# A two-block model on one core: experts' weights read by whole 8 KB rows, gate and up in two PSUM banks each, and the second block's small loads issued by ACT

## The chip, the cores and the metric

The kernel runs on one core of a Trainium2 chip. The metric is the device time of one execution, in microseconds (us). The engines are PE (matrix products), DVE, ACT and POOL (elementwise work), and SP, which here only issues transfers; ACT can issue transfers too. The 16 DMA engines of the core move data between the chip's DRAM and SBUF for both queues.

## The reference

Two transformer blocks follow each other on 256 tokens of width 1024, in float32. The first block (272 tokens with 16 meta tokens) has attention and a convolution, then an expert layer: each of 16 experts chooses its 34 best tokens. The second block has four branches, a merge and a plain feed-forward layer. The expert layer is the part that matters here:

```python
def expert_choice_ffn(h, w_router, w_gate, w_up, w_down):
    cap = EC_CAPACITY_FACTOR * L // N_EXPERTS                  # 34
    logits = jnp.einsum('ld,de->le', hs, w_router)
    aff = jax.nn.softmax(logits, axis=-1)
    g, idx = lax.top_k(aff.T, cap)
    xg = hs[idx]                                               # 16 x 34 x 1024
    a = jnp.einsum('ecd,edf->ecf', xg, w_gate)                 # w_gate 16 x 1024 x 2048
    u = jnp.einsum('ecd,edf->ecf', xg, w_up)                   # w_up   16 x 1024 x 2048
    y = jnp.einsum('ecf,efd->ecd', jax.nn.silu(a) * u, w_down) # w_down 16 x 2048 x 1024
    out = jnp.zeros((L, D)).at[idx.reshape(-1)].add((y * g[..., None]).reshape(-1, D))
```

## The kernel before, in words

The program has three stages, one after the other: block 1, the 16 experts, block 2. The order of instructions on each engine is not the order of the code: the framework schedules the program when it is built, by a timeline of its own, and its pools decide which buffer a tile gets.

**Loads of weights.** Every weight matrix is read in pieces of at most 1 MB by `load` (L121, on SP's queue) into a tile `raw` of 128 partitions x 2048 floats, that is 8 KB to a partition. There are 18 such tiles during the experts (12 from the start, 4 and 2 more when block 1 gives up space). A load waits until the tile's last reader is done. It also waits for a semaphore: all transfers of SP's and ACT's queues share eight, named DMAHW0 to DMAHW7 in the program's order, handed out in turn as the scheduler places the transfers, and a transfer waits until the one that had its semaphore before has landed. So no more than eight transfers are on their way, counted over both queues.

**Experts** (`moe`, from L728). `xg` holds the chosen tokens of eight experts, transposed, with 34 columns padded to 64. It is made by `gather` (L715, five products `gat_p` for each of the eight 128-row blocks K of the model width, then a copy to `xg`), once ahead of expert 0 and once inside expert 7. A product of an expert (`pair`, L737) takes 64 columns of `xg` against 1024 weight columns as two products of 512 columns, one into each half of the partitions. For each expert and each half `fh` of the 2048 hidden columns: four loads of `w_gate` (a load holds 256 model rows x 1024 hidden columns), eight pairs into one PSUM bank `pg`; four loads of `w_up`, eight pairs into `pu`; the banks are copied to SBUF (`sg` on ACT, `su` on DVE), transposed on PE (`gT_p`, four 128x128 pieces), passed through Silu on ACT (`sl`) and multiplied on DVE to `hT`. Then eight loads of `w_down` feed 16 pairs into `py`; ACT copies it to `ys`, PE spreads it over the tokens (`cmb_p`), DVE adds it to `hres`. An expert has 24 loads of 1 MB: 8 gate, 8 up, 8 down.

**Small loads of block 2** (`params2`, L851). Norm gains, biases and tables of block 2 are loaded by 21 small transfers on SP's queue. Seven go to tiles of their own (`c_inv`, `r_alog`, `r_dtb`, `r_fb`, `r_gqr`, `r_gkr`, `r_sgb`) and the scheduler places them in block 1. Fourteen reuse tiles that the second `gather` reads last (`c_tri`, eleven rows of `p_rows`, `p_sgw`, `p_pos`) and are placed after it.

Of the kernel before, what the change touches and what calls it, by code (L numbers as in the profile page):

```python
# [7 lines left out]
F32 = mybir.dt.float32  # L8
# [717 lines left out]
def moe(g, pc):  # L726
# [4 lines left out]
    with ExitStack() as c:  # L731
# [7 lines left out]
        for e in range(g.NEXP):  # L739
            if e == 0:  # L740
                places(g, 0)
                gather(g, ps)
                last = weigh(g, 0)
            if e == min(8, g.NEXP - 1):
                with tc.issue_after(last.ins):
                    q2 = params2(g, pc)
            if e == min(10, g.NEXP - 1):
                with tc.issue_after(g.last.ins), tc.issue_after(g.lastv.ins):
                    params2_calc(g, q2, *(ps.tile([128, 512], F32, tag="mt", name="ws_p") for _ in range(2)))

            sT_p = ps.tile([128, 512], F32, tag="mt", name="sT_p")
            for i in range(2):
                for n in range(2):
                    nc.tensor.matmul(
                        sT_p[HALF[n], i * 128 : i * 128 + 128], g.Sg[:, i, e % 8], g.ident, start=True, stop=True
                    )
            sT = wk.tile([128, 256], F32, tag="sT", name="sT")
            nc.vector.tensor_copy(sT, sT_p[:, :256])
            hT = wk.tile([128, 16, 64], F32, tag="hT", bufs=1, name="hT")
            for fh in range(2):  # L760
                for nm, weights in (("g", I["w_gate"]), ("u", I["w_up"])):
                    p = ps.tile([128, 512], F32, tag="p" + nm, bufs=1, name="p" + nm)
                    for kq in range(4):
                        w = load(
                            g,
                            weights[0, e, kq * 256 : kq * 256 + 256, fh * 1024 : fh * 1024 + 1024].rearrange(
                                "(k p) f -> p k f", p=128
                            ),
                            2,
                            1024,  # L770
                        )
                        for kk in range(2):
                            K = kq * 2 + kk
                            pair(p, g.xg[:, K, e % 8], w[:, kk], K == 0, K == 7)
                    s = wk.tile([128, 512], F32, tag="s", name="s" + nm)
                    if nm == "g":
                        nc.scalar.activation(s, p, AF.Copy)  # L777
                    else:
                        nc.vector.tensor_copy(s, p)  # L779
                    pt = ps.tile([128, 512], F32, tag="mt", name="gT_p")  # L780
                    for j in range(4):
                        js = slice(j * 128, j * 128 + 128)
                        nc.tensor.transpose(pt[:, js], s[:, js], g.ident)

                    if nm == "g":
                        sl = wk.tile([128, 512], F32, tag="sl", name="sl")
                        nc.scalar.activation(sl, pt, AF.Silu)
                    else:
                        h = hT[:, fh * 8 : fh * 8 + 8].rearrange("p (n j) c -> p j n c", n=2)
                        pv, sv = (x.rearrange("p (j n c) -> p j n c", j=4, n=2) for x in (pt, sl))  # L790
                        nc.vector.tensor_tensor(h, sv, pv, op=ALU.mult)
            if e == 7:
                places(g, 1)
                gather(g, ps)
                last = weigh(g, 1)
            py = ps.tile([128, 512], F32, tag="py", bufs=2, name="py")
            for q in range(8):
                w = load(g, I["w_down"][0, e, q * 256 : (q + 1) * 256].rearrange("(k p) f -> p k f", p=128), 2, 1024)
                for kk in range(2):
                    K = q * 2 + kk  # L800
                    pair(py, hT[:, K], w[:, kk], K == 0, K == 15)
            ys = wk.tile([128, 512], F32, tag="s", name="ys")
            g.last = nc.scalar.activation(ys, py, AF.Copy)  # L803
            for i in range(2):
                pn = [ps.tile([128, 512], F32, tag="mt", name="cmb_p") for _ in range(2)]
                for n in range(2):
                    ins = nc.tensor.matmul(pn[n], sT[HALF[n], i * 128 : i * 128 + 128], ys[HALF[n]], start=True, stop=True)  # L807
                for n in range(2):
                    d = g.h[:, i, n * 512 : (n + 1) * 512]
                    g.lastv = nc.vector.tensor_tensor(d, pn[n], d, op=ALU.add)  # L810
# [39 lines left out]
def params2(g, pool):  # L850

    nc, I = g.nc, g.I
    q = Ctx()
    dma = nc.sync.dma_start

    def row(name, src, n):
        t = pool.tile([128, n], F32, name="r_" + name)
        dma(t, src.broadcast_to([128, n]))
        return t

    q.inv = load_const(g, pool, "inv")
    q.tri0 = load_const(g, g.rt, "tri", tag="hh1")
    q.rows = g.rt.tile([98, 128], F32, tag="hl0", name="p_rows")
    nc.gpsimd.memset(q.rows, 0.0)
    q.vec = pool.tile([128, 98], F32, name="p_vec")
# [1066 lines left out]
```

## Time and profile before

| what | value |
|---|---|
| median of 3 runs | 1705.66 us (1704.28 to 1706.36) |
| profiled execution, device time | 1703.82 us |
| its span, first to last instruction | 1702.0 us |
| PE busy | 1517.8 us, 89% of the span |
| DVE, ACT, POOL busy | 583.4, 438.8, 128.0 us |
| moved by DMA | 510.65 MB, of which 384 loads of 1 MB are the experts' weights |

The profiled execution is 1.84 us below the median of the runs. The span is the time from the first to the last instruction. The busy time of an engine counts neither its waits nor the transfers that it issues. The profile also has, for each stretch of time, the busy share of the 16 DMA engines, the rate at which they moved data and the clock granted to PE as a part of its full speed.

### The profile page before, as it was taken

How to read it: one execution, taken by the hardware profiler on the slowest of the kernel's cores; microseconds unless marked ns; L12 is line 12 of the kernel's file. 1: busy time of each engine (PE TensorE's matmuls, PEld its weight loads, DVE VectorE, ACT ScalarE, POOL GpSimd, SP SyncE). 2: the span in 40 equal slices, each digit the busy share in tenths (PEclk: the TensorE clock that was granted, in tenths of full speed). 3: DMA queues.
4: the chain of work that ended last, by engine and by line, in shares of the span. 5: the costliest groups of instructions: out<-in, count | busy, mean ns of one | idle time of the engine just before them, and what ended most of it. 6: DMA issues, size and time to landing. Idle time of an engine off the chain costs nothing.

```text
span 1702.0 us, 21226 instructions
## 1 busy us (share of the span) xinstructions
PE 1517.8 (89%) x8652; PEld 889.3 (52%) x8652; DVE 583.4 (34%) x1071; ACT 438.8 (26%) x882; POOL 128.0 (8%) x134
## 2 busy tenths in 40 slices
PE   7999999978878897878888887869999999999999
PEld 6887333222222232222222222228999998989998
DVE  5675111101101110101110110127888765576554
ACT  3544100000000000000000000026677444455543
POOL 2043000000000000000000000010141111220000
PEclk8999999999999999999999999999999999999999
DMA  9746899999999999999999999984442433466653
GB/s 291 230 135 237 323 409 409 409 409 410 409 409 409 409 409 344 409 409 409 408 409 409 409 409 409 409 315 149 151 154 75 149 125 112 137 197 199 197 186 113
DMA packets 189736, 510.65 MB, mean 300 GB/s; under 512 B 10827, under 2 KB 80438, under 8 KB 189638
## 3 DMA queue, kind: packets, MB, share of 16 engines
q1 hardware_dynamic: 188118, 509.01, 79.5%
q8 instruction: 68, 1.11, 0.3%
q10 hardware_dynamic: 1520, 0.28, 0.1%
q14 instruction: 30, 0.25, 0.0%
HBM read 508.21 MB, written 1.05 MB: 299 GB/s over the span
## 4 chain that ended last, share of the span: by engine, by line
PE 45%; DMA 42%; DVE 2%; issue 1%; ACT 0%; POOL 0%; SPq 0%; ACTq 0%; DVEq 0%; POOLq 0%
DMA raw<-in_w_up_dram 28%; DMA raw<-in_w_down_dram 14%; PE pu L737 5%; PE py L737 4%; PE pg L737 3%; PE pA_p L1079 3%; PE pA_p L1081 3%; PE pA_p L1080 3%; PE ff_p L1823 2%; PE ff L1862 2%; PE ff L1861 2%; PE ff_p L1824 2%; PE ff_p L1825 2%; PE ff L1860 2%; PE pB_p L1097 1%; PE pB_p L1099 1%
## 5 line engine op out<-in xcount | busy, mean ns | idle before, releaser
L150 DVE TENSOR_TENSOR wl<-raw,wh 128x1024 fp32r<-128x1024 f32 (+4 forms) x212 | 246.2, 1163 | 128.8 <-ACT wh L148 128.1
L737 PE MATMUL py<-raw,hT 128*64 128x512 f32 x1024 | 244.3, 602 | 47.1 <-DMA raw<-in_w_down_dram 47.1
L737 PE MATMUL pu<-raw,xg 128*64 128x512 f32 x1024 | 248.8, 607 | 41.8 <-DMA raw<-in_w_up_dram 41.5
L148 ACT ACTIVATE wh<-raw 128x1024 fp32r<-128x1024 f32 (+4 forms) x214 | 208.4, 976 | 199.0 <-PE pA_p L1080 42.5
L737 PE MATMUL pg<-raw,xg 128*64 128x512 f32 x1024 | 242.7, 600 | 15.6 <-DMA raw<-in_w_gate_dram 15.6
L737 PEld LDWEIGHTS py<-raw,hT 128*64 128x64 f32 x1024 | 66.2, 136 | 208.4 <-issue 105.8
L779 DVE COPY su<-pu 128x512 f32<-128x512 f32 x32 | 22.1, 692 | 438.5 <-PE pu L737 438.5
L737 PEld LDWEIGHTS pu<-raw,xg 128*64 128x64 f32 x1024 | 65.8, 137 | 199.2 <-DMA raw<-in_w_up_dram 108.5
L810 DVE TENSOR_TENSOR hres<-cmb_p,hres 128x512 f32<-128x512 f32 x64 | 41.2, 686 | 333.5 <-PE cmb_p L807 333.5
L737 PEld LDWEIGHTS pg<-raw,xg 128*64 128x64 f32 x1024 | 66.1, 136 | 159.9 <-issue 109.0
L803 ACT ACTIVATE ys<-py 128x512 f32<-128x512 f32 x16 | 9.6, 597 | 422.1 <-PE py L737 422.1
L777 ACT ACTIVATE sg<-pg 128x512 f32<-128x512 f32 x32 | 19.1, 597 | 376.2 <-PE pg L737 376.2
L1081 PE MATMUL pA_p<-x2h,wl 128*128 128x256 f32 x384 | 109.5, 285 | 0.0
L1079 PE MATMUL pA_p<-x2h,wh 128*128 128x256 f32 x384 | 109.3, 285 | 0.2 <-ACT abk L1722 0.2
L1080 PE MATMUL pA_p<-x2l,wh 128*128 128x256 f32 x384 | 108.1, 281 | 0.0
L1079 PEld LDWEIGHTS pA_p<-x2h,wh 128*128 128x128 f32 x384 | 72.4, 189 | 2.0 <-issue 0.8
L1081 PEld LDWEIGHTS pA_p<-x2h,wl 128*128 128x128 f32 x384 | 72.2, 188 | 2.1 <-issue 1.9
L1080 PEld LDWEIGHTS pA_p<-x2l,wh 128*128 128x128 f32 x384 | 72.3, 188 | 1.1 <-issue 0.8
L1824 PE MATMUL ff_p<-fl,wh 128*128 128x256 f32 x256 | 71.1, 279 | 0.0
L1823 PE MATMUL ff_p<-fh,wh 128*128 128x256 f32 x256 | 70.1, 278 | 0.8 <-ACT fh L1002 0.5
L1825 PE MATMUL ff_p<-fh,wl 128*128 128x256 f32 x256 | 70.5, 277 | 0.0
L461 PE MATMUL proj_p<-xh,wh 128*128 128x272 f32 x192 | 57.4, 313 | 1.9 <-DVE hT L282 1.9
(574 smaller groups left out, 2282.3 us busy)
## 6 DMA issues: line engine op xcount, KB each, us to landing
raw<-in_w_gate_dram SPq DMA_DIRECT2D x128, 1024.0 KB
raw<-in_w_up_dram SPq DMA_DIRECT2D x128, 1024.0 KB
raw<-in_w_down_dram SPq DMA_DIRECT2D x128, 1024.0 KB
raw<-in_w_in_dram SPq DMA_DIRECT2D x43, 1024.0 KB
raw<-in_w_ff_dram SPq DMA_DIRECT2D x32, 1024.0 KB
raw<-in_w_out_dram SPq DMA_DIRECT2D x8, 1024.0 KB
raw<-in_w_branch_dram SPq DMA_DIRECT2D x16, 512.0 KB
raw<-in_w_in_dram SPq DMA_DIRECT2D x4, 512.0 KB
```

What stands on the lines that cost most here:

```text
L148: g.lastw = nc.scalar.activation(h, x, AF.Copy)
L150: ve.tensor_tensor(l, x, h.bitcast(F32), op=ALU.subtract)
L461: ins = nc.tensor.matmul(p[:, :L1], w[:, k, js], x[:, k], start=(n == 0), stop=(n == 23))
L737: nc.tensor.matmul(p[HALF[n]], x, w[:, n * 512 : n * 512 + 512], start=first, stop=last)
L810: g.lastv = nc.vector.tensor_tensor(d, pn[n], d, op=ALU.add)
L1079: nc.tensor.matmul(o, wh[:, k, js], xh[:, k], start=(k == 0), stop=False)
L1080: nc.tensor.matmul(o, wh[:, k, js], xl[:, k], start=False, stop=False)
L1081: nc.tensor.matmul(o, wl[:, k, js], xh[:, k], start=False, stop=(k == 7))
L1823: nc.tensor.matmul(o, wh[:, k, js], fh[:, k], start=(k == 0), stop=False)
L1824: nc.tensor.matmul(o, wh[:, k, js], fl[:, k], start=False, stop=False)
L1825: nc.tensor.matmul(o, wl[:, k, js], fh[:, k], start=False, stop=(k == 7))
L1860: nc.tensor.matmul(o, a[:, TS[t]], wh[:, j, ns], start=(K == 0), stop=False)
```

## The change

It has three parts. Rows: the gate and up loads take 128 whole rows of 2048 floats, so each partition receives one run of 8 KB in place of two runs of 4 KB; the down loads give each partition two neighbouring rows of 4 KB, again one run of 8 KB. Banks: a gate or up load now holds all 2048 hidden columns of one K, so both halves are summed side by side, `pg` and `pu` are two PSUM banks each, all eight gate loads come ahead of all eight up loads, and the copies and transposes of the two halves follow each other; the transposes read `s` in another order, so that the rows of `hT` match the new rows of the down loads. Small loads: all 21 of `params2` are issued by ACT in place of SP.

```diff
-            for fh in range(2):
-                for nm, weights in (("g", I["w_gate"]), ("u", I["w_up"])):
-                    p = ps.tile([128, 512], F32, tag="p" + nm, bufs=1, name="p" + nm)
-                    for kq in range(4):
-                        w = load(
-                            g,
-                            weights[0, e, kq * 256 : kq * 256 + 256, fh * 1024 : fh * 1024 + 1024].rearrange(
-                                "(k p) f -> p k f", p=128
-                            ),
-                            2,
-                            1024,
-                        )
-                        for kk in range(2):
-                            K = kq * 2 + kk
-                            pair(p, g.xg[:, K, e % 8], w[:, kk], K == 0, K == 7)
+            sls = []
+            for nm, weights in (("g", I["w_gate"]), ("u", I["w_up"])):
+
+                p = ps.tile([128, 2, 512], F32, tag="p" + nm, bufs=1, name="p" + nm)
+                for K in range(8):
+                    w = load(
+                        g,
+                        weights[0, e, K * 128 : K * 128 + 128].rearrange("p (a f) -> p a f", a=2),
+                        2,
+                        1024,
+                    )
+                    for fh in range(2):
+                        pair(p[:, fh], g.xg[:, K, e % 8], w[:, fh], K == 0, K == 7)
+                for fh in range(2):
...
+                    sv = s.rearrange("p (m q k) -> p m k q", m=2, k=2)
                     for j in range(4):
-                        js = slice(j * 128, j * 128 + 128)
-                        nc.tensor.transpose(pt[:, js], s[:, js], g.ident)
+                        nc.tensor.transpose(pt[:, j * 128 : j * 128 + 128], sv[:, j // 2, j % 2], g.ident)
...
-                w = load(g, I["w_down"][0, e, q * 256 : (q + 1) * 256].rearrange("(k p) f -> p k f", p=128), 2, 1024)
+                w = load(g, I["w_down"][0, e, q * 256 : (q + 1) * 256].rearrange("(p k) f -> p k f", k=2), 2, 1024)
...
-    dma = nc.sync.dma_start
+
+    dma = nc.scalar.dma_start
...
-    q.inv = load_const(g, pool, "inv")
-    q.tri0 = load_const(g, g.rt, "tri", tag="hh1")
+    q.inv = load_const(g, pool, "inv", eng=nc.scalar)
+    q.tri0 = load_const(g, g.rt, "tri", tag="hh1", eng=nc.scalar)
```

Three places of the built program show what moved. In brackets stands what an instruction waits for; x4 is four equal rows.

The first place is ACT near the start of the program, where `xh` is block 1's input, transposed and scaled. Before:

```order
L251 ACTIVATE sqx,ssx<-hres 128x1024 [waits Pool_49]
L261 ACTIVATE xh<-ptx,mg 128x272 [waits DVE_49,PE_49]
L261 ACTIVATE xh<-ptx,mg 128x272 [waits PE_49] x3
L148 ACTIVATE wh<-raw 128x1024 [waits DMAHW4_49]
L261 ACTIVATE xh<-ptx,mg 128x272 [waits PE_49] x3
```

The same place of ACT after the change:

```order
L251 ACTIVATE sqx,ssx<-hres 128x1024 [waits Pool_49]
L93 DMA c_inv<-in_consts_dram 128x32 [waits DMAHW5_49]
L860 DMA r_alog<-in_dn_a_log_dram 128x4 [waits DMAHW7_49]
L261 ACTIVATE xh<-ptx,mg 128x272 [waits DVE_49,PE_49]
L261 ACTIVATE xh<-ptx,mg 128x272 [waits PE_49]
L860 DMA r_dtb<-in_dn_dt_bias_dram 128x4 [waits DMAHW1_49]
L261 ACTIVATE xh<-ptx,mg 128x272 [waits PE_49] x5
L148 ACTIVATE wh<-raw 128x1024 [waits DMAHW4_49]
L275 ACTIVATE sqx,ssx<-hres 128x1024 [waits DMAHW2_49,Activation_49]
L860 DMA r_fb<-in_fox_f_bias_dram 128x4 [waits DMAHW4_49]
```

Two small loads now stand ahead of the first `xh`, one between them, and four more (`r_fb` to `r_sgb`) ahead of the eighth `xh`.

The second place is expert 8, after the second gather. On SP before, the fourteen small loads stood between the sixth and the seventh load of the second half's rows of `w_up`, each waiting for the semaphore of a transfer eight places ahead:

```order
L121 DMA raw<-in_w_up_dram 128x2x1024 [waits DMAHW5_49,PE_49]
L93 DMA c_tri<-in_consts_dram 128x128 [waits DVE_49,DMAHW6_49,PE_49,Pool_49]
L870 DMA p_rows<-in_norm_g_dram 8x128 [waits DMAHW7_49,Pool_49]
...
L899 DMA p_pos<-in_positions_dram 2x128 [waits DMAHW3_49,PE_49]
L121 DMA raw<-in_w_up_dram 128x2x1024 [waits DMAHW4_49,PE_49]
```

On ACT after the change they stand between the last copy of the gather (`xg`) and `ys` of expert 7:

```order
L896 DMA p_sgw<-in_sg_w_s_dram 128x4x128 [waits DMAHW6_49,PE_49]
L721 ACTIVATE xg<-gat_p,vec 128x8x34 [waits PE_49]
L93 DMA c_tri<-in_consts_dram 128x128 [waits DMAHW7_49]
...
L872 DMA p_rows<-in_mla_q_norm_g_dram 2x128 [waits DMAHW5_49]
...
L901 DMA p_pos<-in_positions_dram 2x128 [waits DMAHW6_49]
L804 ACTIVATE ys<-py 128x512 [waits DVE_49,PE_49]
```

SP after the change has only weight loads there; these are the last three up loads of expert 8 and its first two down loads, with the semaphores left to them:

```order
L121 DMA raw<-in_w_up_dram 128x2048 [waits DMAHW5_49,PE_49]
L121 DMA raw<-in_w_up_dram 128x2048 [waits DMAHW2_49,PE_49]
L121 DMA raw<-in_w_up_dram 128x2048 [waits DMAHW6_49,PE_49]
L121 DMA raw<-in_w_down_dram 128x2048 [waits DMAHW2_49,PE_49]
L121 DMA raw<-in_w_down_dram 128x2048 [waits DMAHW7_49,PE_49]
```

The semaphores missing from this row of loads (3, 4, 5, 7, 0, 1, and so on) went to the small loads of ACT.

The third place is PE in the first gather, where `pg` and `pu` begin (`Sm,hm` is the last of the five gather products of a K, `hh` and `hl` are the high and low part of the tokens). Before, each K has two gate and two up products after its gather:

```order
L715 MATMUL gat_p<-S,hl_1943 128x272
L715 MATMUL gat_p<-Sm,hm 128x272
L737 MATMUL pg<-raw,xg 64x512 x2
L737 MATMUL pu<-raw,xg 64x512 x2
L715 MATMUL gat_p<-S,hh_1936 128x272
```

After the change:

```order
L715 MATMUL gat_p<-S,hl_1943 128x272
L715 MATMUL gat_p<-Sm,hm 128x272
L737 MATMUL pg<-raw,xg 64x512 x4
L737 MATMUL pu<-raw,xg 64x512 x4
L715 MATMUL gat_p<-S,hh_1936 128x272
...
L737 MATMUL pg<-raw,xg 64x512 x2
...
L737 MATMUL pg<-raw,xg 64x512 x6
L737 MATMUL pu<-raw,xg 64x512 x2
```

K = 0 now has four products of each kind, since a load holds both halves of its K; behind the third gather six gate products of K = 1 and 2 come ahead of the next up products.

Block 1's first products and the middle of block 2 (attention, the delta rule and the merge) also stand in another order on PE, DVE and ACT, with the same instructions.

## Rows read from the trace of the kernel before

**Rows 1.** The page: GB/s in 40 equal slices of the span.

```profile
GB/s 291 230 135 237 323 409 409 409 409 410 409 409 409 409 409 344 409 409 409 408 409 409 409 409 409 409 315 149 151 154 75 149 125 112 137 197 199 197 186 113
```

**Rows 2.** The chain that ended last, us 321 to 362: start, length, what.

```profile
321.50 18.66 DMA raw<-in_w_up_dram
...
341.99 18.62 DMA raw<-in_w_up_dram
```

**Rows 3.** Windows: busy of PE, PEld, DVE, ACT, POOL (instructions), PE's clock, DMA share, GB/s.

```profile
20.00:50.00 30.00, 29.60 (x211) 27.64 (x211) 19.50 (x39) 11.66 (x24) 6.31 (x7) 0.96 1.09 348
200.00:300.00 100.00, 99.24 (x466) 35.12 (x464) 11.43 (x18) 7.06 (x12) 0.00 (x0) 1.00 1.03 409
700.00:1100.00 400.00, 328.38 (x1467) 95.78 (x1465) 42.26 (x78) 19.77 (x35) 0.00 (x0) 1.00 1.03 409
...
1200.00:1700.00 500.00, 495.50 (x3512) 453.59 (x3510) 325.60 (x577) 264.88 (x532) 68.73 (x60) 1.00 0.47 149
```

**Rows 4.** DMA packets in us 30 to 40, and in us 500 to 520.

```profile
DMA packets 3450, 3.48 MB, mean 348 GB/s; under 512 B 55, under 2 KB 3450, under 8 KB 3450
...
DMA packets 2115, 8.17 MB, mean 408 GB/s; under 512 B 125, under 2 KB 125, under 8 KB 2113
```

**Rows 5.** Windows in single loads of block 2, columns as in rows 3.

```profile
1512.75:1514.25 1.50, 1.50 (x8) 1.23 (x7) 0.65 (x1) 0.37 (x1) 0.00 (x0) 1.00 1.03 423
...
1415.50:1417.00 1.50, 1.50 (x10) 1.19 (x9) 0.93 (x1) 1.11 (x2) 0.24 (x1) 1.00 1.07 380
```

**Rows 6.** DMA packets around those two loads, us 1512.5 to 1514.5 and 1415 to 1417.

```profile
DMA packets 205, 0.84 MB, mean 420 GB/s; under 512 B 0, under 2 KB 0, under 8 KB 205
...
DMA packets 725, 0.74 MB, mean 371 GB/s; under 512 B 0, under 2 KB 725, under 8 KB 725
```

**Rows 7.** Windows around the small loads of expert 8, columns as in rows 3.

```profile
660.00:666.00 6.00, 5.24 (x26) 1.45 (x22) 0.00 (x0) 1.19 (x2) 0.00 (x0) 1.00 0.38 144
666.00:674.00 8.00, 0.61 (x4) 0.29 (x4) 0.00 (x0) 0.00 (x0) 0.00 (x0) 0.82 0.85 259
674.00:680.00 6.00, 5.32 (x16) 1.31 (x12) 0.63 (x1) 0.00 (x0) 0.00 (x0) 0.67 1.03 416
```

**Rows 8.** Timeline of SP's queue there: start, us, line, what was issued.

```profile
656.42 0.22 SPq L870 DMA_DIRECT2D p_rows<-in_dn_out_norm_g_dram  x1
658.98 0.23 SPq L870 DMA_DIRECT2D p_rows<-in_mla_q_norm_g_dram  x1
...
666.66 0.91 SPq L121 DMA_DIRECT2D raw<-in_w_up_dram  x2
```

**Rows 9.** Timeline of PE: expert 7's end, a stall in expert 8, the last expert.

```profile
626.54 7.09 PE L737 MATMUL py<-raw,hT 128*64 128x512 f32 x32
634.39 1.13 PE L807 MATMUL cmb_p<-ys,sT 64*128 64x512 f32 x4 [0.76 <-ACT ys L803]
...
673.46 5.86 PE L737 MATMUL pu<-raw,xg 128*64 128x512 f32 x16 [7.39 <-DMA raw<-in_w_up_dram]
...
1129.27 1.94 PE L737 MATMUL py<-raw,hT 128*64 128x512 f32 x8 [0.64 <-DMA raw<-in_w_down_dram]
```

**Rows 10.** Timelines of PE and SP's queue in the first gather.

```profile
171.66 1.08 PE L737 MATMUL pg<-raw,xg 128*64 128x512 f32 x4
...
175.66 0.37 SPq L121 DMA_DIRECT2D raw<-in_w_down_dram  x1
```

**Rows 11.** Start of the program: SP's wait, and timelines of ACT, DVE and PE.

```profile
SPq L419 <- DMA gw<-in_w_router_dram: 1.0, 1, 1.0
...
11.47 0.35 SPq L419 DMA_DIRECT2D lamv<-in_lambda_k_dram  x1
8.80 1.62 ACT L261 ACTIVATE xh<-ptx,mg 128x272 fp32r<-128x272 f32 x4 [0.44 <-PE ptx L260]
11.69 2.25 DVE L521 CAST tri<-c_tri 128x128 bf16<-128x128 f32 x1 [1.05 <-DMA c_tri<-in_consts_dram]
17.96 2.15 PE L461 MATMUL proj_p<-xh,wh 128*128 128x272 f32 x8 [1.92 <-DVE hT L282]
```

More of the change, by code (lines that the diff above doesn't have):

```diff
@@ L759, in moe @@
             hT = wk.tile([128, 16, 64], F32, tag="hT", bufs=1, name="hT")
-            for fh in range(2):
-                for nm, weights in (("g", I["w_gate"]), ("u", I["w_up"])):
-                    p = ps.tile([128, 512], F32, tag="p" + nm, bufs=1, name="p" + nm)
-                    for kq in range(4):
-                        w = load(
-                            g,
-                            weights[0, e, kq * 256 : kq * 256 + 256, fh * 1024 : fh * 1024 + 1024].rearrange(
-                                "(k p) f -> p k f", p=128
-                            ),
-                            2,
-                            1024,
-                        )
-                        for kk in range(2):
-                            K = kq * 2 + kk
-                            pair(p, g.xg[:, K, e % 8], w[:, kk], K == 0, K == 7)
+            sls = []
[11 more added lines that the diff above has]
+                for fh in range(2):
                     s = wk.tile([128, 512], F32, tag="s", name="s" + nm)
                     if nm == "g":
-                        nc.scalar.activation(s, p, AF.Copy)
+                        nc.scalar.activation(s, p[:, fh], AF.Copy)
                     else:
-                        nc.vector.tensor_copy(s, p)
+                        nc.vector.tensor_copy(s, p[:, fh])
                     pt = ps.tile([128, 512], F32, tag="mt", name="gT_p")
+                    sv = s.rearrange("p (m q k) -> p m k q", m=2, k=2)
                     for j in range(4):
-                        js = slice(j * 128, j * 128 + 128)
-                        nc.tensor.transpose(pt[:, js], s[:, js], g.ident)
+                        nc.tensor.transpose(pt[:, j * 128 : j * 128 + 128], sv[:, j // 2, j % 2], g.ident)
                     if nm == "g":
@@ L787, in moe @@
                         nc.scalar.activation(sl, pt, AF.Silu)
+                        sls.append(sl)
                     else:
                         h = hT[:, fh * 8 : fh * 8 + 8].rearrange("p (n j) c -> p j n c", n=2)
-                        pv, sv = (x.rearrange("p (j n c) -> p j n c", j=4, n=2) for x in (pt, sl))
+                        pv, sv = (x.rearrange("p (j n c) -> p j n c", j=4, n=2) for x in (pt, sls[fh]))
                         nc.vector.tensor_tensor(h, sv, pv, op=ALU.mult)
```

## The prediction

> **What bounds the kernel now.** I read the rate row of the page first: from the fifth slice to the 26th the DMA engines move 409 GB/s almost throughout, and in the last quarter 75 to 199 [rows 1]. So the experts are a stretch of transfers, and block 2 is something else. The windows say what: in us 700 to 1100 PE is busy 328 of 400 us while the DMA share is 1.03, in us 1200 to 1700 PE is busy 495.5 of 500 with the DMA engines at half share [rows 3]. The chain confirms it for the experts: transfer stands behind transfer, and the next link begins 341.99 - 321.50 = 20.49 us after the one before [rows 2]. Eight transfers are in flight, each waits for the one eight places ahead, so a load of 1 MB costs 20.49 / 8 = 2.56 us, which is 1.0486 MB at 409 GB/s. Eight products of PE that use one load take 1.94 us [rows 9], so PE waits 0.6 us for each; the last expert's last load is reached at 1129.27 after such a wait. What shortens a load by x shortens the experts by x times the number of loads that are bound so; what shortens PE there is worth nothing.
>
> How many are bound so: an expert has 24 loads, 16 experts 384. The first 18 are fetched into the free tiles in block 1, and about 8 follow at the pace at which the first gather gives tiles back. The other 358 run at the DMA rate. In us 200 to 300 PE still works off what was fetched ahead (99.24 of 100 us busy), but the rate is 409 there too, so these loads count [rows 3].
>
> **The rate.** The change halves the number of pieces of a load: 256 of 4 KB become 128 of 8 KB, for each of the 16 DMA engines 16 become 8. No row shows 8 KB pieces, so the price of a piece comes from smaller ones. In us 20 to 50 block 1 loads its weights at 348 GB/s [rows 3], and there the pieces are of 1 KB: 3450 for 3.48 MB; in the experts they are of 4 KB, 2115 less 125 small ones for 8.17 MB [rows 4]. At 348 GB/s 1 MB takes 3.013 us, at 409.3 2.562 us; an engine handles 64 pieces in the first and 16 in the second, so 48 pieces make 0.451 us, 9.4 ns a piece. Eight fewer give 0.075 us: a load takes 2.487 us, 421.6 GB/s, and 358 loads save 26.9 us. The lower end is nothing, if the 61 GB/s between the stages have another cause than the size of the pieces; the upper end is the whole cost of the present 16 pieces, 16 x 9.4 ns x 358 = 54 us. A second pair of rows gives a smaller price: in single loads of block 2, 1.5 us from the middle of each, 423 GB/s with 4 KB pieces and 380 with 1 KB [rows 5, 6]. That is 2.479 against 2.759 us for 1 MB, 5.8 ns a piece, 0.047 us a load, 16.7 us in all. I take the first pair, since it is of sustained streams as the experts are, and keep the second as a rival.
>
> The Trainium skill, page "DMA: Bandwidth & Descriptors", section "Why small descriptors are slow (HBM only)", names a fixed overhead of about three cycles for each packet and 32 bytes of metadata for each operation, and says that joining descriptors is only worth it up to 256 bytes. By the figures of that page's section "Where 436 GB/s comes from" (850 MHz, 32 bytes a cycle) I estimate 4.7 ns a piece from it, and 13 us for this change; the rows on 1 KB pieces disagree with the limit of 256 bytes.
>
> **The small loads of expert 8.** Before, fourteen small loads stand in SP's queue, and each waits for a semaphore that a weight load holds: they are issued 2.56 us apart (656.42, 658.98), and the next weight load only at 666.66 [rows 8]. The queue of transfers runs dry: 144 GB/s in us 660 to 666 and 259 in 666 to 674, against 409 [rows 7], (265 x 6 + 150 x 8) / 409 = 6.8 us lost. PE waits 7.39 us there [rows 9]. All of this goes.
>
> Afterwards the loads stand on ACT and wait just so. `p_sgw` stands ahead of the last `xg` and waits for a gate load of expert 8; `p_pos`, the last, waits for DMAHW6, which the eighth up load of expert 8 holds (third order piece of the second place). Behind it stands `ys` of expert 7. So `ys`, wanted when expert 7's last down load is used up, goes only when 16 further loads have landed: 16 x 2.49 = 40 us, less about 4 us of products that PE still has (two loads at 1.94 us); `cmb_p`, which now follows `ys` with a wait of 0.76 us [rows 9], and all of PE behind it stand still for some 36 us. SP runs on meanwhile, but a tile comes free only with a product: 18 loads after the last one used the tiles are full. When the 16 have passed, two loads (5.0 us) are still in hand. A tile comes free 0.76 + 1.13 + 1.94 = 3.8 us later (`ys`, `cmb_p`, the first products [rows 9]), and a load into it starts at most 4.2 us after that: before, from the issue at 666.66 to the first use at 673.46 were 6.8 us [rows 8, 9], of which 2.56 are the load itself. So transfers pause for 3.8 + 4.2 - 5.0 = 3.0 us at most, 0 at least; I take 3.0, since that start was measured at this place. PE restarts at a lower clock: after its stall of 7.39 us the granted clock was 0.82, then 0.67 for 6 us [rows 7], that is 4 us at 1.2 GHz in place of 2.4 and 2 us of products late; 1.4 of them I add, the rest falls into the pause. The small loads' own transfers no longer lie in a gap: 0.36 MB at 409 GB/s and 40 pieces of 512 bytes an engine at 9.4 ns, 0.9 + 0.4 = 1.3 us. Lost 5.7 us in place of 6.8: -1.1. Range: -5, if no transfer pauses, to +8, if PE's slow restart holds the tiles for several loads.
>
> **The head.** `c_inv` and `r_alog` now stand ahead of the first `xh` on ACT. `r_alog` waits for `gw`; SP saw that wait end at 11.47 (its `lamv`), while `xh` began at 8.80 [rows 11]. With its issue behind it (0.35 us for `lamv`) `xh` starts near 11.9, 3.1 us late. What hangs on it is the DVE work on the same tokens and the first projection on PE at 17.96, which waits 1.92 us for DVE's `hT`. DVE has slack: it waits 1.05 us at 11.69 and then casts a constant for 2.25 us, which it can do first. I take half, +1.6 us; 0 if the cast covers it, +4 if `r_dtb` between the `xh` holds ACT again. Block 1 behind it is PE's (29.60 of 30 us busy [rows 3]), so this passes on whole.
>
> **The first gather.** SP's first expert load behind the full tiles was issued at 175.66, when K = 1's gate products (two behind those of K = 0, which start at 171.66) freed a tile [rows 10]. Now the load of K = 0 holds both halves, four `pg` rows in place of two, and its tile is free at about 173.5, while the later ones come no faster (six gate products between two gathers, as the third place shows). So one load starts 2 us sooner, of which I count -0.7, between -2 and +2.
>
> **Nothing.** Seven small loads leave SP's queue in block 1, where PE is busy throughout [rows 3]; if that cover went, 7 x 0.23 us of issue [rows 8] would count, 1.6 us. The copies of two banks in a row make `gT_p` of `su` come later by one copy and four transposes, which I put at no more than the products of a load, 1.94 us [rows 9]; `hT` is then late for the down products, and the 0.6 us a load that PE waits anyway take it up over four loads. Without that cover it would be 1.94 x 16 = 31 us, but then PE would have to be the bound, which its 82% deny. The strided transposes have the same number and size. Block 2 is PE's with 99% busy [rows 3]; its other order moves no work: 0, kept as -4 to +6.
>
> **Sum:** -26.9 - 1.1 + 1.6 - 0.7 = -27.1. The profiled execution took 1703.8 us, 1.8 under the median, so 1676.7 for a profiled one and 1678.6 by the median of before. Parts other than the rate make -0.2 together.
>
> **Rivals.** A smaller price of a piece, 5.8 ns, as the single loads have it: 1705.7 - 16.7 - 0.2 = 1688.8. For it: the two rows differ in nothing but the size. Against: neither is sustained. 0.17.
> No change of the rate: the 409 GB/s are what the memory or the engines' ports give whatever the pieces, and 348 in block 1 is block 1's own. For it: 409 stands without a tenth of change over 20 slices [rows 1]. Against: 423 in one load of the same pieces [rows 5]. 1705.7 - 0.2 = 1705.5; 0.12. The Trainium skill, same page and section "Where 436 GB/s comes from", lets the memory side bind at about 358 GB/s, by which the pieces would matter nothing; the 409 of the trace disagrees with that figure.
> A larger gain: the sustained stream comes to what a single load reaches, 2.479 - 0.047 = 2.432 us; 0.130 x 358 = 46.5 us, 1659.0. 0.06.
> Slower: the stall at expert 8. After it PE is 18 loads behind, and the remaining some 150 loads come at PE's pace, if that is the slower. The 27 us are gone when 150 x (p - 2.49) exceeds them, from p = 2.67 us a load on; with p = 2.75, 39 us are lost: 1717. For it: at 1.2 GHz 1.94 us become 3.9. Against: in us 200 to 300 PE did 466 products where us 700 to 1100 have 1467 for 156 loads, so 50 loads in 100 us, 2.0 us a load [rows 3]; and after the stall of 7.39 us PE was at 1.2 GHz for only about 4 of 6 us [rows 7]. 0.05.
>
> **How the numbers follow.** The forecast, 1678.6, has 0.57, and by its other terms 1670 to 1687 as a range of its own; 0.03 is left for mishaps, a third to each sign. The range that should hold 8 in 10 takes in the forecast, the smaller price and the larger gain, and leaves out no change and the stall, 0.17, and some of the mishaps: 1657 to 1697. A change of 0.2%, 3.4 us, is about what a measurement of this kernel tells from none. Faster are 0.57 + 0.17 + 0.06, 0.02 of the no-change case, whose head and stall may come out either way, and 0.01: 0.83. The same are 0.08 of that case and 0.01, slower its last 0.02, the stall and 0.01: 0.09 and 0.08.
>
> **What would show it.** The rate row at 421 or 422 in the experts, and loads 2.49 us apart; the last expert's last load used near 1102. ACT held and PE idle for about 36 us between 610 and 655, with less than 6 us of missing transfers, and 2.0 us a load behind it. The first projection at 19.5, the first down load issued at 173.5. From the last load to the end as long as now, about 573 us. The prediction is wrong if the rate stays at 409, if PE's rows behind expert 8 don't wait for loads again within 100 us, or if block 2 has grown.

## The result, and the profile after

The changed kernel takes 1679.63 us (median of 4 runs, 1679.28 to 1681.54) against 1705.07 us before (median of 4 runs; the three ahead of the prediction gave 1705.66): a ratio of 0.9854, 95% interval 0.9842 to 0.9866. That is 25.4 us faster; 1678.6 us was forecast. The profiled execution has a span of 1678.1 us, against 1702.0.

The page of the changed kernel, PE's granted clock in tenths and GB/s in 40 slices of 42 us:

```profile
PEclk8999999999999996999999999989999999999999
GB/s 275 260 137 234 336 420 420 419 420 420 419 420 421 420 420 340 413 420 420 419 420 421 420 420 420 420 249 163 167 117 89 139 126 126 120 202 196 199 192 110
```

Where [rows 1] have 409, there is now 420. One slice in the middle has 340 (344 before) and a clock of 6 tenths. Windows of the changed kernel, columns as in rows 3:

```profile
20.00:50.00 30.00, 30.00 (x219) 27.72 (x218) 21.52 (x44) 12.95 (x26) 8.31 (x9) 0.99 1.09 348
200.00:300.00 100.00, 98.04 (x453) 36.45 (x454) 11.26 (x18) 6.95 (x12) 0.00 (x0) 1.00 1.01 420
700.00:1100.00 400.00, 352.09 (x1603) 113.14 (x1599) 42.42 (x80) 20.80 (x38) 0.00 (x0) 1.00 1.01 420
...
900.00:1000.00 100.00, 84.24 (x376) 25.68 (x376) 11.18 (x18) 3.47 (x6) 0.00 (x0) 1.00 1.01 420
```

They answer to [rows 3]. Block 1, whose pieces are still of 1 KB, has the same 348 GB/s. The experts have 420 in place of 409. PE is busy 352 of 400 us in place of 328, for the most part because until us 843 it works off the loads that pile up in a stall shown below; in us 900 to 1000, behind that, it is busy 84.24 of 100. It is still not the bound. The DMA packets in us 500 to 520 and one link of the chain in the same stretch:

```profile
DMA packets 1153, 8.40 MB, mean 420 GB/s; under 512 B 128, under 2 KB 128, under 8 KB 128
...
511.62 19.87 DMA raw<-in_w_up_dram
531.55 19.87 DMA raw<-in_w_down_dram
```

Less the 128 small ones, 1025 packets carry the 8.40 MB: 8 KB each, where [rows 4] had 4 KB. The link is 19.93 us for eight loads, 2.491 us each, against 2.561 us by [rows 2]. So 8 pieces fewer gave 0.070 us: 8.7 ns a piece. The place where the stall was forecast, as windows (same columns); behind the first dots stands the whole stretch, behind the second the same stretch of the kernel before:

```profile
640.00:650.00 10.00, 0.00 (x0) 0.00 (x0) 0.00 (x0) 0.00 (x0) 0.00 (x0) 0.50 1.03 408
650.00:655.00 5.00, 0.00 (x0) 0.00 (x0) 0.00 (x0) 0.00 (x0) 0.00 (x0) 0.50 0.73 268
655.00:659.00 4.00, 2.91 (x6) 0.80 (x8) 0.80 (x2) 0.60 (x1) 0.00 (x0) 0.50 1.00 420
659.00:664.00 5.00, 5.00 (x14) 1.32 (x12) 1.18 (x2) 0.00 (x0) 0.00 (x0) 0.66 0.25 70
664.00:666.00 2.00, 2.00 (x10) 0.43 (x6) 0.00 (x0) 0.00 (x0) 0.00 (x0) 1.00 0.97 410
666.00:674.00 8.00, 8.00 (x45) 3.06 (x46) 1.02 (x2) 0.00 (x0) 0.00 (x0) 1.00 0.91 311
...
600.00:660.00 60.00, 25.86 (x110) 10.42 (x107) 2.86 (x6) 2.56 (x5) 0.20 (x1) 0.71 0.98 399
660.00:700.00 40.00, 38.11 (x174) 13.34 (x173) 4.30 (x7) 2.28 (x4) 0.00 (x0) 0.97 0.91 360
...
600.00:660.00 60.00, 55.65 (x262) 20.99 (x264) 7.77 (x13) 4.59 (x9) 0.20 (x1) 1.00 1.03 409
660.00:700.00 40.00, 27.62 (x114) 7.91 (x110) 1.38 (x2) 1.79 (x3) 0.00 (x0) 0.91 0.89 341
```

And the timeline there, of ACT, PE and SP, with the stall of PE:

```profile
631.39 0.40 ACTq L896 DMA_DIRECT2D p_sgw<-in_sg_w_s_dram  x1
655.10 0.24 ACTq L901 DMA_DIRECT2D p_pos<-in_positions_dram  x1
655.44 0.60 ACT L804 ACTIVATE ys<-py 128x512 f32<-128x512 f32 x1 [23.12 <-DMA raw<-in_w_up_dram]
...
656.09 2.08 PE L808 MATMUL cmb_p<-ys,sT 64*128 64x512 f32 x4 [34.14 <-ACT ys L804]
...
652.65 0.80 SPq L121 DMA_DIRECT2D raw<-in_w_down_dram  x2
...
661.80 0.33 SPq L121 DMA_DIRECT2D raw<-in_w_down_dram  x1
```

`ys` stands behind `p_pos`, and PE waits 34.14 us for it at the lower clock (0.50). Transfers go on at 408 GB/s for most of that and fall only from 650 on. Against 420, us 600 to 660 (399 GB/s) and 660 to 700 (360) are short by (21 x 60 + 60 x 40) / 420 = 8.7 us of transfers: 1.8 us of them in us 650 to 655, 4.2 in 659 to 664, 2.1 in 666 to 674, and 0.6 in all the rest. Against 409, the same windows of before (409, then 341) were short by 6.7 us.

For a ledger I cut each span in three: up to the first gather (`gat_p` on PE: 168.42 before, 166.25 after), the experts (up to the last load's products on PE: 1129.27 in [rows 9], 1103.20 after), and the rest, which is block 2.

```profile
166.25 0.36 PE L715 MATMUL gat_p<-S,hh 128*128 128x272 f32 x1 [0.23 <-DVE S L687]
1103.20 1.94 PE L737 MATMUL py<-raw,hT 128*64 128x512 f32 x8 [0.56 <-DMA raw<-in_w_down_dram]
```

| kernel | block 1 | experts | block 2 | span | median |
|---|---|---|---|---|---|
| before | 168.4 | 960.9 | 572.7 | 1702.0 | 1705.1 |
| after | 166.3 | 937.0 | 574.9 | 1678.1 | 1679.6 |
| small loads on SP (e1) | 168.6 | 933.2 | 571.5 | 1673.3 | 1676.1 |
| before, small loads on ACT (e2) | 166.2 | 958.5 | 570.8 | 1695.5 | 1698.1 |
| down by 4 KB (e3) | 167.9 | 945.0 | 574.2 | 1687.1 | 1687.1 |
| small loads on POOL (e4) | 169.9 | 931.7 | 571.0 | 1672.6 | 1675.1 |
| seven on ACT, rest POOL (e5) | 167.9 | 930.9 | 574.4 | 1673.2 | 1673.9 |
| all 21 on ACT behind `ys` (e8) | 170.3 | 936.3 | 571.5 | 1678.1 | 1680.1 |
| seven on SP, rest POOL (e9) | 168.0 | 930.1 | 572.2 | 1670.3 | 1673.1 |

The whole gain, 23.9 us of span, lies in the experts; block 1 is 2.2 us shorter and block 2 2.2 us longer, and they cancel. The stages of a kernel come from one profiled execution each, and the runs of one kernel lie up to 3.8 us apart (1685.07 to 1688.91 for e3); so 2 or 3 us of one stage in one kernel are a hint, unless several kernels show them.

### The profile page after: what moved, and what is told of

It reads as the page before. It is cut to its first block, busy times and chain, and to the rows that moved or that the text cites. A ratio compares the mean times of both kernels' runs of the same rounds, so it can differ in the third digit from the quotient of the medians.

```text
span 1678.1 us, 21265 instructions
## 1 busy us (share of the span) xinstructions
PE 1513.0 (90%) x8652; PEld 908.6 (54%) x8652; DVE 578.5 (34%) x1071; ACT 436.7 (26%) x882; POOL 128.9 (8%) x134
## 4 chain that ended last, share of the span: by engine, by line
PE 48%; DMA 40%; DVE 2%; issue 1%; ACT 1%; POOL 0%; SPq 0%; ACTq 0%; DVEq 0%
DMA raw<-in_w_up_dram 14%; DMA raw<-in_w_down_dram 13%; DMA raw<-in_w_gate_dram 12%; PE pg L737 5%; PE pu L737 4%; PE py L737 4%; PE pA_p L1081 3%; PE pA_p L1083 3%; PE pA_p L1082 3%; PE ff_p L1825 2%; PE ff L1864 2%; PE ff L1863 2%; PE ff_p L1827 2%; PE ff_p L1826 2%; PE ff L1862 2%; PE pB_p L1101 1%
## 5 line engine op out<-in xcount | busy, mean ns | idle before, releaser
L737 PE MATMUL pu<-raw,xg 128*64 128x512 f32 x1024 | 240.9, 600 | 23.0 <-DMA raw<-in_w_up_dram 22.9
L737 PE MATMUL py<-raw,hT 128*64 128x512 f32 x1024 | 234.9, 598 | 25.1 <-DMA raw<-in_w_down_dram 21.0
L808 PE MATMUL cmb_p<-ys,sT 64*128 64x512 f32 x128 | 40.8, 659 | 44.8 <-ACT ys L804 43.2
```

The lines of the kernel that those rows point to most:

```text
L737: nc.tensor.matmul(p[HALF[n]], x, w[:, n * 512 : n * 512 + 512], start=first, stop=last)
```

## The experiments

Each was timed beside the kernel before, in three groups (e1 to e4, e5 to e8, e9), where that kernel had medians of 1705.6, 1706.1 and 1704.5 us. Between rows of the table that differ by under 3 us I read the stages, with the caution above.

**The small loads back on SP.** The rows and the banks alone.

```diff
-    dma = nc.scalar.dma_start
+    dma = nc.sync.dma_start
-    q.inv = load_const(g, pool, "inv", eng=nc.scalar)
-    q.tri0 = load_const(g, g.rt, "tri", tag="hh1", eng=nc.scalar)
+    q.inv = load_const(g, pool, "inv")
+    q.tri0 = load_const(g, g.rt, "tri", tag="hh1")
```

> The whole change but for the small loads, which SP issues as before. In the changed kernel the stretch at expert 8 lost 8.7 us of transfers against 6.7 before, the first gather began 2.2 us sooner and block 2 was 2.2 us longer. Theory A (the rows make the gain, the small loads on ACT cost 2.0 us at expert 8, and the shifts of block 1 and block 2 come with the other order of small loads and cancel): 1679.6 - 2.0 = 1677.6. Theory B (the shift of block 1 comes from the small loads on ACT and that of block 2 does not): 1679.6 - 2.0 + 2.2 = 1679.8. Theory C (part of the gain comes from the small loads on ACT, as the stall of 7.4 us of PE is gone from SP's queue): 1685 or more.

1676.14 us, ratio 0.9828 (0.9815 to 0.9842): not slower than the whole change, by the medians 3.5 us faster. Theory C falls. A's number is the nearer, but not by its reasons: block 1 is 2.3 us longer than in the changed kernel (as in B), the experts 3.8 us shorter, block 2 3.4 us shorter. Its windows at expert 8 are short of 420 GB/s by 39 x 60 / 420 = 5.6 us:

```profile
600.00:660.00 60.00, 53.39 (x246) 20.41 (x248) 5.41 (x10) 4.84 (x9) 0.20 (x1) 0.98 0.93 381
660.00:700.00 40.00, 33.80 (x152) 10.47 (x150) 5.58 (x9) 0.60 (x1) 0.00 (x0) 0.99 1.01 422
```

**The small loads on ACT alone**, in the kernel before (the same lines of `params2` as in the change).

> The kernel before, with nothing changed but the small loads, which ACT issues. Theory A (worth a loss of 2.0 us at expert 8 and nothing else): 1705.1 + 2.0 = 1707. Theory B (block 1 is 2.2 us shorter with them, block 2 unchanged): 1704.9. Theory C (they make part of the gain): 1700 or less. In each case ACT is held some 40 us at expert 8 and PE stands still for over 30 us.

1698.05 us, ratio 0.9960 (0.9947 to 0.9974): 7.5 us faster, which is C's side and neither A nor B. The stages say how: block 1 -2.3, experts -2.3, block 2 -1.9. PE stands still as forecast, and yet less is lost than before:

```profile
600.00:660.00 60.00, 29.39 (x136) 11.82 (x132) 3.38 (x6) 1.97 (x4) 0.20 (x1) 0.79 1.03 407
660.00:700.00 40.00, 30.73 (x138) 10.38 (x140) 4.38 (x7) 2.99 (x5) 0.00 (x0) 0.85 0.96 364
...
667.65 2.08 PE L807 MATMUL cmb_p<-ys,sT 64*128 64x512 f32 x4 [36.21 <-ACT ys L803]
```

A stall of PE of 36.21 us costs (2 x 60 + 45 x 40) / 409 = 4.7 us of transfers here, 2.0 less than the stall of 7.39 us in [rows 9]. What counts is when transfers pause, not how long PE does. So the move to ACT is worth -7.5 us without the rows and banks and about +3.5 us on top of them: the parts of this change do not add up. That each part sets another order for the rest is the likely reason; it was not traced, but for block 2 (below).

**Down loads by 4 KB again**, with their transposes, the rest as changed.

```diff
-... w_down ... .rearrange("(p k) f -> p k f", k=2), 2, 1024)
+... w_down ... .rearrange("(k p) f -> p k f", p=128), 2, 1024)
...
```

> The changed kernel, but the down loads give a partition two pieces of 4 KB again (the same 1 MB of neighbouring rows). Theory P (a piece costs a fixed time of an engine; measured 2.562 - 2.493 us = 0.0695 us for 8 pieces, 8.7 ns each): 128 of 384 loads, 119 of the 358 that the transfers bind, are 0.0695 us longer: 1679.6 + 8.3 = 1687.9, and the rate in us 200 to 600 is 416 to 417 GB/s. Rival L (the gain is that gate and up loads no longer take every second 4 KB of the rows but one run of memory of 1 MB; the down loads always did): 1679.6, and 420 GB/s.

1687.05 us: 7.4 above the changed kernel, 8.05 in the experts; P said 8.3. The rate in us 200 to 600 is 417. A load is the same 1 MB of neighbouring memory in both, so only the size of the pieces differs, and with it the order in which that memory is read: rival L falls. For the gate and up loads, rows and banks were changed together and not tried apart.

```profile
200.00:600.00 400.00, 352.26 (x1598) 112.02 (x1596) 39.19 (x63) 21.34 (x37) 1.25 (x2) 1.00 1.02 417
```

**Down loads by 2 KB** (e6, small loads on POOL): 512 rows by 512 columns to a load.

```diff
+                n, k0 = q // 4, (q % 4) * 4
...
+                    nc.tensor.matmul(py[HALF[n]], hT[:, K], w[:, kk], start=K == 0, stop=K == 15)
...
```

> The kernel with all small loads on POOL, but a down load takes 512 rows by 512 columns, so each partition gets four pieces of 2 KB: 32 pieces an engine in place of 8. Theory P (a fixed price a piece, 8.4 to 9.4 ns as measured between 8, 16 and 64 pieces): 24 x 8.6 ns = 0.21 us for 119 loads, 1675.1 + 24.6 = 1699.7, down loads at 387 GB/s. Rival (the price is only paid below some size, so 2 KB cost as 4 KB): 1675.1 + 8.0 = 1683.

1748.37 us, far from both. The time is no test of the pieces, since my edit made PE the bound: all products of a load now go to one half of `py`'s partitions. The packets still tell a rate: in us 378 to 381, of 2 KB pieces only, 387 GB/s, P's number. It is a soft one, since other windows of 2 KB pieces have 380 (us 430 to 436) to 397 (us 374 to 377). All lie well below the 409 of 4 KB pieces, which speaks against the rival.

```profile
DMA packets 585, 1.16 MB, mean 387 GB/s; under 512 B 18, under 2 KB 18, under 8 KB 585
...
DMA packets 1138, 2.28 MB, mean 380 GB/s; under 512 B 33, under 2 KB 33, under 8 KB 1137
DMA packets 597, 1.19 MB, mean 397 GB/s; under 512 B 16, under 2 KB 16, under 8 KB 597
...
1087.36 26.02 PE L810 MATMUL py<-raw,hT 128*64 128x512 f32 x64 [0.24 <-DVE hT L792]
```

**Down loads by 16 KB** (e7, small loads on POOL): four neighbouring rows to a partition, 2 MB to a load, three tiles of 16 KB in place of six of 8.

```diff
+                w = g.big[g.nbig % 3].tile([128, 4, 1024], F32, tag="raw2", name="raw2")
+                nc.sync.dma_start(
+                    w, I["w_down"][0, e, q * 256 : (q + 2) * 256].rearrange("(p k) f -> p k f", k=4)
+                )
...
```

> The kernel with all small loads on POOL, but down loads are of 2 MB into three tiles of 16 KB a partition (in the place of six tiles of 8 KB), so that each partition gets one piece of 16 KB: 4 pieces an engine for each MB in place of 8. Theory P (8.6 ns a piece, at any size): 4 x 8.6 ns x 119 = -4.1 us: 1671.0, down loads at 427 GB/s. Rival (above 8 KB a piece costs no less for a MB): 1675.1. A third way: the tiles of 16 KB come free more coarsely and the transfers pause: over 1677.

1680.64 us, so the third way. The rate did rise: 422 against 420 GB/s over us 200 to 600 is 2.485 against 2.497 us for a MB, 0.012 on the mean and 0.036 on the third of the loads that changed; P said 0.034 (from two rounded rates, so this is a rough agreement). It was given back by coarser tiles: PE waits 4.66 us for the last load and then has 9.49 us of products left, where the changed kernel has 1.94. That is 7.6 us, more than the 5.5 us by which this kernel is behind all on POOL (1675.14). Up to the last load the stage was only 0.5 us shorter than there and not 4.1; where the rest of that gain went was not traced.

```profile
200.00:600.00 400.00, 349.31 (x1562) 124.47 (x1558) 36.12 (x58) 17.71 (x32) 0.00 (x0) 0.96 1.01 422
...
1099.35 9.49 PE L738 MATMUL py<-raw,hT 128*64 128x512 f32 x32 [4.66 <-DMA raw<-in_w_down_dram]
```

**All small loads on POOL**, which nothing on PE's path waits for in the experts, and whose transfers have semaphores of their own (in the trace eight others than those of SP's and ACT's transfers).

```diff
-    dma = nc.scalar.dma_start
+    dma = nc.gpsimd.dma_start
...
```

> The changed kernel, but POOL issues the small loads; their semaphores are then others than those of the weight loads, and no engine that PE waits for stands behind them. Theory A (the stall at expert 8 costs the 8.7 us of transfers that were lost there, and only the small loads' own 1.3 us remain): 1679.6 - 7.4 = 1672.2, PE without a wait of more than 5 us in us 600 to 690. Rival (lost transfers are made up elsewhere, so the stall costs nothing): 1679.6.

1675.14 us, 4.5 below the changed kernel; A said 7.4. In the stage itself it is 5.3 us (937.0 to 931.7), and block 1 is 3.6 us longer. At expert 8 PE has no wait above 1.0 us left, and the transfers are 5 x 60 / 420 = 0.7 us short in place of 8.7; so of 8.0 us of transfers won, 5.3 reached the end of the stage, and I did not trace the rest.

```profile
600.00:660.00 60.00, 55.71 (x260) 21.21 (x256) 7.60 (x13) 4.85 (x9) 7.47 (x15) 1.00 1.01 415
660.00:700.00 40.00, 33.89 (x152) 10.35 (x152) 5.60 (x9) 0.60 (x1) 0.00 (x0) 1.00 1.01 420
```

**All 21 on ACT behind `ys` of expert 7**, none in block 1.

```diff
-                with tc.issue_after(last.ins):
+                with tc.issue_after(g.last.ins):
                     q2 = params2(g, pc)
```

> The changed kernel, but all 21 small loads on ACT stand behind expert 7's ys and ahead of expert 8's first sg, none in block 1. PE can then use the eight gate loads of expert 8 before it misses ACT. Theory T (transfers paused in the changed kernel because PE's stall kept the tiles): PE's stall is some 10 us shorter, eight tiles come free in time, and less than 3 us of transfers are lost in us 600 to 700, against 8.7. Theory L (they paused because the small loads took the semaphores, so that fewer weight loads were in flight): SP's down loads wait for DMAHW2 at every second load here, and 8 us or more are lost. Time by T 1680 - 6 + 2 (block 1 as with SP) = 1676 or less, by L 1682.

1680.11 us. PE used its eight gate loads first, but then stood still for 32.6 us all the same (21 loads hold ACT longer than 14). With eight tiles free the transfers still ran dry, 93 GB/s in us 662 to 668; over 600 to 700 they are (420 - 391) x 100 / 420 = 6.9 us short, nearly all of it in us 656 to 674. SP's waits in us 640 to 680 name the cause:

```profile
600.00:700.00 100.00, 64.62 (x296) 25.39 (x298) 10.03 (x17) 4.85 (x9) 0.20 (x1) 0.83 0.96 391
662.00:668.00 6.00, 0.00 (x0) 0.00 (x0) 0.00 (x0) 0.00 (x0) 0.00 (x0) 0.50 0.30 93
...
SPq L121 <- DMA c_tri<-in_consts_dram: 11.4, 1, 11.4
SPq L121 <- DMA r_fb<-in_fox_f_bias_dram: 11.3, 1, 11.3
```

A weight load there waits for the semaphore that a small load got, and the small load waits in ACT's queue. T falls as the whole cause, since 6.9 us and not under 3 are lost, though the stall was not the 10 us shorter that T's test wanted. L's mechanism is shown, at 6.9 us rather than 8. In the changed kernel both happen in turn, by SP's waits in us 640 to 670 (us in total, times, longest): first the semaphore of an up load, then a tile that `pg` holds.

```profile
SPq L121 <- DMA raw<-in_w_up_dram: 19.2, 2, 12.7
SPq L121 <- PE pg L737: 14.1, 3, 8.3
```

**Shared out**: the fourteen on POOL, and the seven of block 1 on ACT (first) or on SP (second).

```diff
-        dma(t, src.broadcast_to([128, n]))
+        nc.scalar.dma_start(t, src.broadcast_to([128, n]))
...
```

> The changed kernel with the small loads shared out: the seven of block 1 on ACT, as in the change, the fourteen of expert 8 on POOL. In the kernels with the seven on ACT the first gather began at 166.2 us (168.4 and 168.6 with them on SP, 169.9 where POOL issues all of them). Theory A (the stages add up: block 1 as with ACT, experts 931.7 us and block 2 571.0 us as with all on POOL): span 1669, time 1671.4. Rival (the 3.7 us of block 1 are the scheduler's other order and are lost again behind it): 1675, as with all on POOL.

> The changed kernel with the seven small loads of block 1 on SP, as before the change, and the fourteen of expert 8 on POOL. PE's rows then stand in the same order as in the kernels with all small loads on SP or all on POOL, whose block 2 took 571.5 and 571.0 us, against 574.4 to 574.9 us where the seven are on ACT. Theory A (block 2's length goes with that order): first gather at 168.5 us, experts 931 us, block 2 571 us: span 1670.5, time 1673.0. Rival (block 2's length differs from run to run, or hangs on something else): block 2 574 us, time 1676.

With ACT 1673.85 us (ratio 0.9814, 0.9799 to 0.9829), with SP 1673.09 us (0.9821, 0.9808 to 0.9834): the two lowest medians, but not to be told apart from each other, nor clearly from all on POOL (1675.14, 0.9809 to 0.9836) or all on SP (1676.14, 0.9815 to 0.9842). The forecast of A failed with ACT: the experts came as expected, but block 1 was 167.9 and not 166.2, and block 2 574.4 and not 571.0. It held with SP: the span is 1670.3 against 1670.5 expected. PE's rows of block 2 stand there word for word as with all loads on SP or on POOL, and block 2 is 572.2, nearer to theirs than to the 574 to 575 of the other order. Over the table, the three kernels with that other order (the changed one, e3, e5) have 574.2 to 574.9, the six with the order of before 570.8 to 572.7. So part of what the small loads do is to make the scheduler choose another block 2. ACT alone does not bring it, since e2 keeps the order of before. Which of its rows costs the 2 to 3 us was not tried.

## Why the prediction was right, and where it was not

**What bounds the kernel.** Right: all that the kernel won, it won in the experts, at the rate of the transfers; the waits of 0.5 to 0.6 us a load are still there ([rows 9] and 1103.20 above). One reading behind it was off, "each waits for the one eight places ahead":

```profile
340.20 1.94 PE L737 MATMUL pu<-raw,xg 128*64 128x512 f32 x8 [0.62 <-DMA raw<-in_w_up_dram]
341.99 2.30 SPq L121 DMA_DIRECT2D raw<-in_w_up_dram  x1
...
531.55 0.33 SPq L121 DMA_DIRECT2D raw<-in_w_down_dram  x1
```

Before, PE already used the load eight places ahead at 340.20, but SP began the next issue only at 341.99, and was then busy with it for 2.30 us: it issued load behind load. In the first gather such an issue took 0.37 us ([rows 10]), so I take it that SP was held up by a full queue of transfers, which leaves the transfers as the bound. After the change an issue takes 0.33 us, and the wait is the one that the prediction describes (the load eight places ahead, issued in the link of 511.62, lands 0.06 us before 531.55).

**The rate**, -26.9 forecast from 9.4 ns a piece: 8.7 ns and 358 x 0.070 = -25.1 us. The pair of rows from sustained streams was the right one; the pair from single loads (5.8 ns) was a third too low. Over all runs the rows make a series: a MB takes 2.491 us in 8 KB pieces (8 an engine), 2.561 in 4 KB (16), 2.71 at the 387 GB/s of 2 KB (32), 3.013 in 1 KB (64), that is 8.7, 9.3 and 9.5 ns for each further piece. The point at 2 KB is soft: by its windows of 380 to 397 GB/s the 9.3 could be 5 to 12 and the 9.5 be 8 to 12. Without it, from 4 KB to 1 KB, it is 9.4. That a piece has a price, with the same memory read, is shown by the 4 KB down loads. The Trainium skill, page "DMA: Bandwidth & Descriptors", section "Why small descriptors are slow (HBM only)", gives the two parts from which 4.7 ns were estimated; the runs show about twice that, and they show a gain well above the 256 bytes to which it limits the joining of descriptors.

**Expert 8**, -1.1 forecast: +2.0, since 8.7 us of transfers were lost and not 5.7. The step that failed is "SP runs on meanwhile, but a tile comes free only with a product": it lets the transfers run at full rate up to one pause, and counts no loss ahead of it or behind it. Ahead of it, 1.8 us were lost: SP's next load, the first down load, waited 6.5 us (19.2 - 12.7 by SP's waits above) for DMAHW2, which the seventh up load held until 652.65, as the order ahead of the prediction has it; the semaphores between had gone to the small loads, and the rate fell to 268 GB/s before `ys` went. Behind it, 2.1 us were lost, at 311 GB/s in us 666 to 674, while each down load waited for a tile that `pg` held. The pause itself came out as forecast in sum, 4.2 us against 3.0 + 1.4, but not in its parts. The two loads "still in hand" were there: issued from 652.65 on, they moved at 420 GB/s in us 655 to 659. The first tile came free 6.7 us after `p_pos` went (655.10 to 661.80) and not 3.8, as `cmb_p` took 2.08 us at the lower clock in place of 1.13, and the products behind it ran at that clock too. The load into it was moving by 664, 2.2 us later and not 4.2. PE's stall itself was as forecast (34.14 us against 36), and so was that it costs little of its length. The clock, 0.50 while PE stood still and 0.66 in us 659 to 664, was back at 1.00 in us 664 to 666, some 8 us after PE's restart.

**The signs.** Of the three signs of being wrong that the prediction names, two came true: block 2 has grown, by 2.2 us, and PE did not wait for a load again within 100 us of expert 8. It did so first at 843.10, 187 us after its restart:

```profile
843.10 1.94 PE L737 MATMUL pu<-raw,xg 128*64 128x512 f32 x8 [0.56 <-DMA raw<-in_w_up_dram]
```

What that second sign was to warn of, experts at PE's pace, did not come: PE used some 87 loads in those 187 us, 2.2 us each, and the transfers ran at 420 GB/s from us 700 on. So working off what had piled up cost no transfers; the limit of 100 us was too short.

**The head**, +1.6 forecast: the first projection came 1.3 us sooner, at 16.68 in place of 17.96. `xh` was late as worked out (11.84), but the step "then casts a constant for 2.25 us, which it can do first" took a duration from a place where the cast waited for something else to end:

```profile
11.51 2.35 POOL L150 TENSOR_TENSOR wl<-raw,wh 128x1024 fp32r<-128x1024 f32 x1 [9.73 <-ACT wh L148]
```

That row of before is POOL's. It ends at 13.86, and DVE's cast in [rows 11] at 13.94 (see the last section). After the change:

```profile
11.84 0.49 ACT L261 ACTIVATE xh<-ptx,mg 128x272 fp32r<-128x272 f32 x1 [3.67 <-DMA gw<-in_w_router_dram]
13.59 0.22 DVE L521 CAST tri<-c_tri 128x128 bf16<-128x128 f32 x1
15.67 2.36 POOL L150 TENSOR_TENSOR wl<-raw,wh 128x1024 fp32r<-128x1024 f32 x1 [13.89 <-DMA r_fb<-in_fox_f_bias_dram]
16.68 2.15 PE L461 MATMUL proj_p<-xh,wh 128*128 128x272 f32 x8 [0.78 <-ACT sqx L275]
```

POOL's `wl` now comes later, and the cast takes 0.22 us. Block 1 as a whole is 2.2 us shorter; the other 0.9 us I did not find, and it is no rule for ACT: with the seven loads on ACT it took 166.2 to 167.9 us, on SP 168.0 to 168.6.

**The first gather**, -0.7 forecast: the first down load was issued 5.2 us after the gather's start (171.46 - 166.25) in place of 7.2 ([rows 10], 175.66 - 168.42). What is left of the experts' -23.9 us after -25.1 and +2.0 is -0.8; it is a remainder and was not measured by itself.

**Nothing**, at block 2: +2.2, within its bounds of -4 to +6 but not nothing; by the table it goes with the scheduler's other order.

**Sum:** -25.1 + 2.0 - 0.8 - 2.2 + 2.2 = -23.9 us of span, against -27.1. It closes because the first gather is a remainder. The forecast's closeness in the end is owed to the rate, 1.8 us less than forecast. Expert 8 and the head had the wrong sign, and together with block 2 their misses (+3.1, -3.8 and +2.2) largely cancel, which is luck.

## What to carry to other kernels

In a stretch that the DMA engines fill, count pieces: each further piece cost about 9 ns of its engine in this kernel (shown best from 4 to 8 KB), and the rate of a stream with other pieces in the same profile gives the price before any run. Small loads that share semaphores with a stream of large ones, on whichever of the two queues, starved the stream here or held the engine that issued them; a queue with semaphores of its own (POOL's) ended that (0.7 us lost in place of 8.7), though its lead of 1.0 us over all on SP is within the noise. A stall of PE is to be priced by the transfers it stops, and a duration is to be taken with a look at what ran beside it.

## What was not expected of the hardware

A DVE cast (128x128, float32 to bf16) that took 0.22 us where POOL did not run took 1.71 to 2.30 us in the seven kernels where it began beside a POOL operation of 2.35 us. In all seven it ended 0.07 to 0.09 us after that operation, however late it had begun: at 13.94 against 13.86 in the kernel before, and in e9 at 13.53 against 13.45.

```profile
11.11 2.34 POOL L150 TENSOR_TENSOR wl<-raw,wh 128x1024 fp32r<-128x1024 f32 x1 [9.32 <-ACT wh L148]
11.82 1.71 DVE L521 CAST tri<-c_tri 128x128 bf16<-128x128 f32 x1 [1.58 <-DMA c_tri<-in_consts_dram]
```

So by these rows it was not slowed down but waited for POOL's end. The Trainium skill, page "GPSIMD Engine Reference", section "1. Specifications", says that POOL shares SBUF interfaces with VectorE, with contention for DVE instructions in a 2-port perf mode or with two SBUF inputs. These rows agree that the two collide; whether this cast, which has one input, is of the first kind no run here shows.

PE's 512-column products with 64 columns of weights took 26.02 / 64 = 0.41 us each where all went to one half of the partitions, and 7.09 / 32 = 0.22 us where they went to the two halves in turn ([rows 9]): neighbours in different halves overlap.
